# Two-layer decoder step on one core: the head gates at the end of the recurrence load into the places of finished chunks, and the prompt's last state leaves on SyncE's queue right behind its last sum

## The chip, the cores and the metric

The kernel runs on one NeuronCore of a Trainium2 chip. The metric is device time in microseconds of one execution. The kernel before took 2952.51 us, the median of three runs (2949.12, 2952.51 and 2954.06 us). Each engine works through its own list of instructions in order: TensorE (PE, with its weight loads shown apart as PEld), VectorE (DVE), ScalarE (ACT) and GpSimd (POOL). DMAs are issued by SyncE (SP), ACT and POOL, and in the trace an engine's issuing side is written SPq or ACTq.

## What is computed

One inference step of a two-layer decoder for a prompt of 1024 tokens (with 16 meta tokens ahead of it) and for 8 samples of 8 tokens, with the same weights. Layer one is an mLSTM, a recurrence over chunks of tokens whose state is a matrix `C` and a vector `n` per head; layer two is attention with forget gates; each is followed by a SwiGLU network. The change lies where layer one's recurrence ends and its output projection begins:

```python
def mlstm_chunk(state, inp):
    C, n, m = state
    ...
    h = num / jnp.maximum(jnp.abs(den), jnp.exp(-m_t))[..., None]
    ...
    C_new = w_c[..., None, None] * C + jnp.einsum('bhs,bhsk,bhsv->bhkv', w_g, k, v)
    n_new = w_c[..., None] * n + jnp.einsum('bhs,bhsk->bhk', w_g, k)
    return (C_new, n_new, m_new), h

def mlstm_mixer(xn, C0, n0, m0, lead, w_in, b_ig, b_fg, mh_g, w_out):
    ...
    h, state = mlstm_sequence(q, k, v, li, lf, state0, lead)
    h = rmsnorm(h.transpose(0, 2, 1, 3), mh_g)
    out = (h.reshape(B, T, HV).astype(xn.dtype) * jax.nn.sigmoid(og)) @ w_out
    return out, state
```

The gate `sigmoid(og)` has 8 heads of 128 columns. The last `C` and `n` of the prompt are outputs of their own, `p_C` and `p_n`.

## The kernel before, in words

**Tiling.** The 1104 tokens are nine tiles: tile 0 holds the 64 sample tokens and the 16 meta tokens, tiles 1 to 8 hold 128 prompt tokens each. Three tiles make a group t (0, 1, 2; 336, 384 and 384 tokens), and the name `vA` stands for the three big tiles, one for each group. A float32 product is made of three matmuls, since every operand is split into a high and a low part: ACT casts the high part (L243), DVE subtracts for the low part (L244), PE runs L170, L171 and L172.

**The recurrence** (`recurrence`, L829) goes through chunks i = 0 to 8, one a tile. For each chunk PE makes scores (`sps`, L998), transposes the keys (`kps`, L1004), makes the state's sum (`cp`, L1037, added to `C` by DVE, L1041) and the outputs (`nps`, L1099 and L1103, copied out by DVE's `den`, L1061, and by ACT into `vA`, L1069). Between these steps `f(n)` runs pieces of other work, above all the projection of the gates (`gates_out`): its results go through ACT's sigmoid into tiles `stg` (three buffers) and out to DRAM as `ogD`. At i = 6 that work is used up (`f(1000)`), and from then on the filler `g` is one head of the gating: a call of `gate` (L666) takes one pair (t, h), group 0 first, and runs `gate_head`: three PE transposes of the normed output into PSUM (`ghps`, L1198, two buffers), a multiplication with the gate by DVE (L1199), ACT's cast and DVE's subtraction into the operands `x0h`/`x0l` (group 0) or `x1h`/`x1l` (group 1). DVE works in order, so a head's multiplication holds up all DVE work behind it.

Chunks 7 and 8 have five such calls each: heads (0,0) to (0,4) and then (0,5) to (0,7), (1,0), (1,1). The gate of a head is loaded from `ogD` by POOL (L663) into a tile `ogc`, which is one of the three `stg` buffers, and is kept up to three heads ahead. Since the loads run ahead, the recurrence also loads heads (1,2) and (1,3), which it doesn't gate.

**Its end.** After chunk 8's outputs `last_state` (L904) issues four DMAs on ACT's queue: `p_C` and `p_n`, for each half a of the partitions. `p_n` writes single float32 elements: its source is one column of `C` (64 partitions by 4 elements). Then ACT and DVE norm group 2 (`norm_heads`, L1171 to L1182).

**The output projection** (`mlp`, L377) comes next. Unit (t, m) is 24 matmuls (`pops`) that make 128 output columns m for group t, and DVE adds it into the residual stream (L433), which POOL loads from DRAM into `vA` as soon as that group's heads are transposed (L398, `vA<-hD`). Units (0,0), (0,1) and (0,2) come first, each with two heads of group 1 behind it: (1,2) and (1,3) after the first, (1,4) and (1,5) after the second, and so on. Their gates are loaded again by a second set made by `heads`, into the `ny` buffers of a pool of `mlp` (three buffers, name `ogc` too). That pool takes over memory that the recurrence held, `C` among it. The weights are loaded by SP: columns 0 to 2 ready split (`wo`, L411), column 3 raw (`woraw`, L418) and columns 4 to 7 raw into two `slot` tiles (L418); ACT and DVE split the raw ones.

**What sets the order.** PE's order is fixed by hand throughout. In the recurrence DVE, ACT and POOL are in the order of the code too. SP, and the others in `mlp`'s first part, are ordered by the scheduler. A DMA may also wait for the semaphore of an earlier DMA that it shares a counter with; such a wait stands in the trace like any other.

Of the kernel before, what the change touches and what calls it, by code (L numbers as in the profile page):

```python
# [7 lines left out]
F32 = mybir.dt.float32  # L8
# [8 lines left out]
P = 128  # L17
# [10 lines left out]
NT = len(TT)  # L28
GRP = [(0, 1, 2), (3, 4, 5), (6, 7, 8)]
TS = [(TT[g[0]][0], TT[g[-1]][1]) for g in GRP]  # L30
SL = max(b - a for a, b in TS)
HA, DK, DV = 8, 64, 128
# [477 lines left out]
def _add(cls):  # L510
    def deco(f):
        setattr(cls, f.__name__, f)
        return f

    return deco
# [44 lines left out]
@_add(Net)  # L560
def phase_a(self, vt):
    nc, I, O = self.nc, self.I, self.O
    w_in = I["w_in_a"][0]
    qkD = self.dram.tile([8, P, T], F32, name="qkD")
    ogD = self.dram.tile([8, P, T], F32, name="ogD")
    v = lambda i: vt[i // 3][:, i % 3 * HA * (DV + 1) : (i % 3 + 1) * HA * (DV + 1)].rearrange(
        "p (h d) -> p h d", h=HA)
    with ExitStack() as c3:
        kp = c3.enter_context(self.pool("kA"))
        gates = kp.tile([P, NT, 16], F32, name="gates")  # L570
        tm = kp.tile([P, NT, 104], F32, name="tmA")
        den = kp.tile([P, NT, HA], F32, name="den")
        ssq = kp.tile([P, NT, HA], F32, name="ssqA")
        self.fin = (tm, den, ssq)
        for i in range(NT):
            nc.gpsimd.memset(v(i)[:, :, DV : DV + 1], 1.0)
        nc.gpsimd.memset(gates, 0.0)
        nc.gpsimd.memset(tm[:, 0, :], 0.0)
        nc.gpsimd.memset(den, 1.0)
        nc.gpsimd.memset(ssq, 1.0)  # L580
        st = c3.enter_context(self.pool("stA", bufs=3))
        with ExitStack() as cw, self.pool("ppA0", bufs=4, space=PSUM) as pp:
            self.wpools(cw, 3, 4)
            self.load_x()
            for c in (3, 0, 1, 2):
                c0 = 2 * HA * DK + 256 * c

                def evac(i, m, ps):
                    nc.scalar.copy(v(i)[:m, 2 * c : 2 * c + 2, :DV], ps[:m, :256].rearrange("p (h d) -> p h d", h=2))
                    if c == 3:  # L590
                        nc.scalar.copy(gates[:m, i, :], ps[:m, 256:272])

                self.tm_proj([w_in[:, c0 : c0 + 256]] + ([w_in[:, 3072:3088]] if c == 3 else []), None, pp, "mm0", 4,
                             evac)

        pp = c3.enter_context(self.pool("ppA", bufs=2, space=PSUM))

        self.wpools(c3, 2, 3, side="left")
        self.cache_prep()


        self.woD = []
        for m in range(3):
            d = self.dram.tile([P, 2, KT, P], F32, name=f"woD{m}")
            for z, y in enumerate(self.load_w([I["w_out_a"][0][:, m * P : (m + 1) * P]])):
                nc.gpsimd.dma_start(d[:, z], y.bitcast(F32))
            self.woD.append(d)

        def qk_out():

            for m in range(8):
                wh, wl = self.load_w([w_in[:, m * P : (m + 1) * P]])
                for t, (t0, t1) in enumerate(TS):
                    n = t1 - t0
                    ps = pp.tile([P, 512], F32, name=self.uid("mmA"), tag="mmA")
                    self.fm_cols(ps[:, :n], wh, wl, t)
                    s = st.tile([P, SL], F32, name=self.uid("stg"), tag="stg")
                    nc.scalar.activation(s[:, :n], ps[:, :n], AF.Copy, scale=DK ** -0.5 if m < 4 else 1.0)
                    nc.gpsimd.dma_start(qkD[m, :, t0:t1], s[:, :n])
                    yield  # L620

        with self.pool("rowsA") as rp, self.pool("rowsAp", bufs=2, space=PSUM) as rpp, \
                self.tc.manual_schedule(engines={mybir.EngineType.PE}):
            prep = self.rec_prep(kp, gates, rp, rpp)
            next(prep)
            for x, _ in enumerate(qk_out()):
                if x in (1, 3, 8):
                    next(prep, None)

        def gates_out():  # L630

            get = lambda m, later=None: self.load_w([w_in[:, (16 + m) * P : (17 + m) * P]], later=later)
            ws = [get(0)]
            later = []
            for m in range(8):
                wh, wl = ws[m]
                for t, (t0, t1) in enumerate(TS):
                    n = t1 - t0
                    ps = pp.tile([P, 512], F32, name=self.uid("mmA"), tag="mmA")
                    xh, xl = self.X[t]  # L640
                    if t == 1 and m < 7:
                        ws.append(get(m + 1, later if m else None))
                    for k in range(KT):
                        if k == 6 and later:
                            later.pop()()
                        self.mm3(ps[:, :n], wh[:, k, :], wl[:, k, :], xh[:, k, :], xl[:, k, :], k == 0, k == KT - 1)
                        if k == KT - 1:
                            s = st.tile([P, SL], F32, name=self.uid("stg"), tag="stg")
                            nc.scalar.activation(s[:, :n], ps[:, :n], AF.Sigmoid)
                            nc.gpsimd.dma_start(ogD[m, :, t0:t1], s[:, :n])  # L650
                        yield

        left = {t: list(range(HA)) for t in range(3)}

        def heads(pp, tag, op):
            ready = []
            todo = [(t, h) for t in (0, 1, 2) for h in left[t]]

            def ahead():
                if todo:  # L660
                    t, h = todo.pop(0)
                    og = op(self.uid("ogc"))
                    nc.gpsimd.dma_start(og[:, : TS[t][1] - TS[t][0]], ogD[h, :, TS[t][0] : TS[t][1]])  # L663
                    ready.append(og)

            def gate(t):  # L666
                if not left[t]:
                    return False
                while todo and len(ready) < 3:
                    ahead()  # L670
                self.gate_head(t, left[t].pop(0), v, ready.pop(0), pp, tag)
                return True
            return gate

        self.recurrence(kp, self.rec, v, qkD, gates_out(),
                        lambda: heads(pp, "mmA", lambda n: st.tile([P, SL], F32, name=n, tag="stg")))
    return heads


# [149 lines left out]
def recurrence(self, kp, rec, v, qkD, fill, gate):  # L829


    nc, I, O = self.nc, self.I, self.O
# [7 lines left out]
    C = [kp.tile([P, 4, DV + 1], F32, name=f"C{a}") for a in range(3)]  # L840
    E = mybir.EngineType
    with ExitStack() as cr, self.pool("recAp", bufs=2, space=PSUM) as pp:
# [5 lines left out]
        sets = {1: r0}  # L848
# [19 lines left out]
        with self.pool("rec2") as sets[2], self.pool("rec1", bufs=2) as rp, self.pool("rec3") as sets[0]:  # L868
            R, N = N, load(2)
            f(10)  # L870
            self.chunk_scores(1, R, rp, *args, f)
            self.chunk_decay(2, N, tm, cap)
            N["exp"]()
            g, norm = f, iter(())
            gate = gate()
            for i in range(1, NT):
                N2 = load(i + 2) if i + 2 < NT else None
                if i + 1 < NT:
                    f(12 if i == 1 else 3)
                    self.chunk_scores(i + 1, N, rp, *args, f)  # L880
                next(norm, None)
                g(2)
                self.chunk_state(i, R, *args, wcP, g)
                if N2:
                    self.chunk_decay(i + 2, N2, tm, cap)
                next(norm, None)
                self.chunk_out(i, R, rp, *args, den, ssq, g, exp=N2 and N2["exp"])
                if i == NT - 1:
                    self.last_state(C[i % 2])
                for _ in norm:  # L890
                    pass
                norm = self.norm_heads(i // 3, v, rp) if i % 3 == 2 else iter(())
                if i == 6:

                    f(1000)
                    g = lambda n: gate(0) or gate(1)
                R, N = N, N2
            order.close()
            for _ in norm:
                pass  # L900


@_add(Net)
def last_state(self, C):  # L904

    nc, O = self.nc, self.O
    for a in range(2):
        cs = C[a * 64 : a * 64 + 64]
        nc.scalar.dma_start(O["p_C"][0, 0, a::2].rearrange("j k v -> k j v"), cs[:, :, :DV])
        nc.scalar.dma_start(O["p_n"][0, 0, a::2].rearrange("j k -> k j").unsqueeze(2), cs[:, :, DV:])  # L910


@_add(Net)
# [1622 lines left out]
```

## Time and profile before

| | |
|---|---|
| median of three runs | 2952.51 us |
| profiled execution, its own time | 2952.6 us |
| span of its trace | 2950.9 us |
| mean granted TensorE clock | 0.985 |
| PE busy | 2830.5 us (96%) |
| DVE, ACT, POOL busy | 57%, 39%, 28% |
| DMA | 464.83 MB, mean 158 GB/s |

Times in rows of the trace count from the start of the span. In a timeline row stand start, duration, engine, line, operation, what it writes and reads, and in brackets how long the engine was idle just before and what ended that. A row of waits has the total in us, how often, and the longest one. A row of windows has for a stretch the busy time of PE, PEld, DVE, ACT and POOL with the number of instructions, then the granted clock, the busy share of the DMA engines and GB/s. The stretch that matters here lies between 422 us, where the gates' projection ends, and 480 us, where the output projection runs without stops.

### The profile page before, as it was taken

The numbers are of one execution on the slowest core, as the hardware profiler recorded it, in microseconds if no ns is written. First come the engines' busy times: TensorE is split into PE (matmuls) and PEld (weight loads), VectorE is DVE, ScalarE is ACT, GpSimd is POOL, SyncE is SP. The second block draws the span as 40 slices with busy tenths as digits, with TensorE's granted clock in tenths as the row PEclk, the third lists the DMA queues.
The fourth block names the chain that finished last, engine by engine and source line by source line (L and its number), as shares of the span: only waits on it lengthen the run. The fifth ranks groups of instructions, "written<-read, shape, count | busy, mean of one in ns | idle before, by whom it ended". The sixth has DMA issues, their size and how long they took to land.

```text
span 2950.9 us, 53409 instructions
## 1 busy us (share of the span) xinstructions
PE 2830.5 (96%) x20709; PEld 2707.7 (92%) x20709; DVE 1686.3 (57%) x3292; ACT 1151.0 (39%) x2103; POOL 825.6 (28%) x1230
## 2 busy tenths in 40 slices
PE   8999987999999999999999999999999999999998
PEld 7999876999999999989999888777899999999998
DVE  5032554776766655754355442677467676665565
ACT  5222453332222234443344443777433222224343
POOL 2011232322322311114353200455232322331122
PEclk9999998999999999999999999999999999999999
DMA  8153545334444375655344575534324454436574
GB/s 260 36 138 89 142 134 147 110 121 149 153 152 148 122 241 187 199 181 173 119 161 141 199 279 201 185 128 150 120 77 132 144 165 142 143 123 221 190 249 149
DMA packets 382760, 464.83 MB, mean 158 GB/s; under 512 B 38626, under 2 KB 303802, under 8 KB 381482
## 3 DMA queue, kind: packets, MB, share of 16 engines
q1 hardware_dynamic: 339970, 323.41, 34.5%
q0 software_dynamic: 37776, 135.42, 14.1%
q8 instruction: 163, 2.67, 0.4%
q10 hardware_dynamic: 4760, 2.57, 0.4%
q14 instruction: 91, 0.75, 0.1%
HBM read 325.02 MB, written 136.29 MB: 156 GB/s over the span
## 4 chain that ended last, share of the span: by engine, by line
PE 76%; DVE 6%; ACT 3%; issue 3%; DMA 2%; POOL 1%; SPq 0%; ACTq 0%; DVEq 0%; POOLq 0%
PE m L1256 22%; PE dps L1571 15%; PE fps L172 4%; PE fps L171 4%; PE fps L170 4%; PE tmps L170 3%; PE tmps L171 3%; PE tmps L172 3%; PE pops L172 2%; PE pops L170 2%; PE pops L171 2%; PE sp L2323 1%; DVE s L2327 1%; PE op L2410 1%; PE bps L170 1%
## 5 line engine op out<-in xcount | busy, mean ns | idle before, releaser
L244 DVE TENSOR_TENSOR slot<-slot,slot 128x1024 fp32r<-128x1024 f32 (+1 forms) x152 | 191.9, 1264 | 123.7 <-ACT slot L243 123.6
L243 ACT CAST slot<-slot 128x1024 fp32r<-128x1024 f32 (+1 forms) x152 | 152.8, 1007 | 188.5 <-PE dps L1571 84.4
L172 PE MATMUL fps<-x0h,slot 128*128 128x336 f32 x688 | 218.2, 317 | 1.6 <-DVE slot L244 1.6
L170 PE MATMUL fps<-x0h,slot 128*128 128x336 f32 x688 | 218.4, 317 | 0.0
L171 PE MATMUL fps<-x0l,slot 128*128 128x336 f32 x688 | 217.4, 316 | 0.0
L1256 PE MATMUL m<-x2h,slot 128*128 128x384 f32 x704 | 193.7, 336 | 0.0
L1256 PE MATMUL m<-x1h,slot 128*128 128x384 f32 x672 | 184.7, 336 | 0.0
L172 PEld LDWEIGHTS fps<-x0h,slot 128*128 128x128 f32 x688 | 129.1, 188 | 2.1 <-DVE slot L244 2.1
L170 PEld LDWEIGHTS fps<-x0h,slot 128*128 128x128 f32 x688 | 129.3, 188 | 0.6 <-ACT slot L243 0.3
L171 PEld LDWEIGHTS fps<-x0l,slot 128*128 128x128 f32 x688 | 129.5, 188 | 0.3
L1256 PEld LDWEIGHTS m<-x2h,slot 128*128 128x128 f32 x704 | 128.5, 188 | 0.0
L1256 PEld LDWEIGHTS m<-x1h,slot 128*128 128x128 f32 x672 | 122.5, 188 | 0.0
L1571 PE MATMUL dps<-T_1h,slot 128*128 128x384 f32 x448 | 119.3, 340 | 2.4 <-ACT T_1h L243 2.4
L1571 PE MATMUL dps<-T_2h,slot 128*128 128x384 f32 x448 | 119.0, 341 | 0.7 <-ACT T_2h L243 0.7
L1256 PE MATMUL m<-x2l,slot 128*128 128x384 f32 x352 | 118.5, 337 | 0.0
L244 DVE TENSOR_TENSOR slot<-vA,slot 128x1024 fp32r<-128x1024 f32 x59 | 83.6, 1417 | 54.8 <-ACT slot L243 54.8
L244 DVE TENSOR_TENSOR slot<-Ht,slot 128x1024 fp32r<-128x1024 f32 x59 | 83.6, 1418 | 54.5 <-ACT slot L243 54.5
L1256 PE MATMUL m<-x1l,slot 128*128 128x384 f32 x336 | 112.8, 336 | 0.0
L316 POOL TENSOR_TENSOR ns<-ns,nq 128x384 f32<-128x384 f32 (+1 forms) x68 | 75.0, 1104 | 133.0 <-ACT nq L314 130.7
L1256 PE MATMUL m<-T_2h,slot 128*128 128x384 f32 x352 | 97.8, 338 | 1.9 <-DVE slot L244 1.9
L2350 ACT ACTIVATE s<-s,nb 128x272 f32<-128x272 f32 (+7 forms) x126 | 98.9, 786 | 0.0
L1256 PE MATMUL m<-T_4h,slot 128*128 128x384 f32 x352 | 97.8, 338 | 0.0
(767 smaller groups left out, 9173.1 us busy)
## 6 DMA issues: line engine op xcount, KB each, us to landing
slot<-in_w_down SPq DMA_DIRECT2D x48, 512.0 KB, 4.6
slot<-in_w_gate_up SPq DMA_DIRECT2D x36, 512.0 KB, 4.3
ws<-in_w_down SPq DMA_DIRECT2D x88, 192.0 KB, 2.9
sD<-ws SPq DMA_DIRECT2D x88, 192.0 KB, 2.2
kp<-in_cache_k SPq DMA_DIRECT2D x32, 512.0 KB, 5.8
vp<-in_cache_v SPq DMA_DIRECT2D x32, 512.0 KB, 5.1
hr<-hB_T POOLq DMA_DIRECT2D x40, 384.0 KB, 5.0
vA<-in_w_gate_up SPq DMA_DIRECT2D x26, 512.0 KB, 3.9
```

Of the source, the lines that this page charges most:

```text
L170: mm(ps, sh, mh, start=first, stop=False)
L171: mm(ps, sh, ml, start=False, stop=False)
L172: mm(ps, sl, mh, start=False, stop=last)
L243: self.nc.scalar.copy(hi, src)
L244: self.nc.vector.tensor_tensor(out=lo, in0=src, in1=hi.bitcast(F32), op=ALU.subtract)
L316: (nc.vector if x >= late else nc.gpsimd).tensor_tensor(out=s, in0=s, in1=sq, op=ALU.add)
L1256: nc.tensor.matmul(u.ps[b], w[p][:, k], x[q][:, k], start=first and k == i == 0, stop=k == 3 and i == 2, skip_group_check=True)
L1571: nc.tensor.matmul(o, p[:, k, ms], q[:, k], start=fresh and k == x == 0, stop=last and k == nk - 1 and x == 2, skip_group_check=True)
L2323: nc.tensor.matmul(ps[z][:, :n], a[r, qs], b[r, at : at + n], start=(y == 0), stop=(y == 2))
L2327: nc.vector.tensor_tensor_reduce(out=ss[z, u][:, at + o : at + e], in0=ps[z][:, o:e], in1=diag[x][:, z] if y else ncb[:, z, at + o : at + ...
L2350: nc.scalar.activation(ss[z, u], ss[z, u], AF.Exp, bias=nb[:, z : z + 1], accum_out=sm[:, u, z : z + 1])
L2410: mm(po[ds[z], :256], vr[:, j0 + x, ds[z]], th[:, x, z], start=(j0 + x == 0), stop=False)
```

## The change

Lines in the changed kernel are 2 lower down in `heads` and up to 18 lower down from `recurrence` on (L663 is L665, L909 and L910 are L927 and L928, L1041 is L1059, L1199 is L1217).

- At i = 6 and i = 7, behind the chunk's outputs, the places of the chunk's `qk` and `eb` tiles are taken over: a new tile of the same tag, halved, gives two places for gates, so four places an iteration, named `ogqk` and `ogeb`. `gate(-1)` loads into all free places and gates nothing.
- In the recurrence `heads` is given this list of places in the place of the `stg` buffers. It loads whenever a place is free, a used place comes free one head later, and exactly ten heads are loaded (`some`).
- `last_state` runs behind chunk 8's `chunk_state`, and its four DMAs are issued by SP.

```diff
-        def heads(pp, tag, op):
-            ready = []
-            todo = [(t, h) for t in (0, 1, 2) for h in left[t]]
+        left[-1] = [None]
+
+        def heads(pp, tag, op=None, some=None):
+
+            ready, used = [], []
+            todo = [(t, h) for t in (0, 1, 2) for h in left[t]][:some]
 
             def ahead():
                 if todo:
                     t, h = todo.pop(0)
-                    og = op(self.uid("ogc"))
+                    og = op(self.uid("ogc")) if callable(op) else op.pop(0)
                     nc.gpsimd.dma_start(og[:, : TS[t][1] - TS[t][0]], ogD[h, :, TS[t][0] : TS[t][1]])
                     ready.append(og)
 
             def gate(t):
                 if not left[t]:
                     return False
-                while todo and len(ready) < 3:
+                while todo and (len(ready) < 3 if callable(op) else op):
                     ahead()
-                self.gate_head(t, left[t].pop(0), v, ready.pop(0), pp, tag)
+                if t < 0:
+                    return False
+                og = ready.pop(0)
+                self.gate_head(t, left[t].pop(0), v, og, pp, tag)
+                if not callable(op):
+
+                    used.append(og)
+                    if len(used) > 1:
+                        op.append(used.pop(0))
                 return True
             return gate
 
         self.recurrence(kp, self.rec, v, qkD, gates_out(),
-                        lambda: heads(pp, "mmA", lambda n: st.tile([P, SL], F32, name=n, tag="stg")))
+                        lambda places: heads(pp, "mmA", places, 10))
...
-            gate = gate()
+            places = []
+            gate = gate(places)
...
                 self.chunk_state(i, R, *args, wcP, g)
+                if i == NT - 1:
+                    self.last_state(C[i % 2])
...
                 self.chunk_out(i, R, rp, *args, den, ssq, g, exp=N2 and N2["exp"])
-                if i == NT - 1:
-                    self.last_state(C[i % 2])
...
                 norm = self.norm_heads(i // 3, v, rp) if i % 3 == 2 else iter(())
+                if i in (6, 7):
+
+                    for x in ("qk", "eb"):
+                        y = sets[i % 3].tile([P, 1024], F32, name=f"og{x}{i}", tag=x,
+                                             bufs=2 if x == "eb" and i == 7 else None)
+                        places += [y[:, z : z + SL] for z in (0, 512)]
+                    gate(-1)
...
-        nc.scalar.dma_start(O["p_C"][0, 0, a::2].rearrange("j k v -> k j v"), cs[:, :, :DV])
-        nc.scalar.dma_start(O["p_n"][0, 0, a::2].rearrange("j k -> k j").unsqueeze(2), cs[:, :, DV:])
+        nc.sync.dma_start(O["p_C"][0, 0, a::2].rearrange("j k v -> k j v"), cs[:, :, :DV])
+        nc.sync.dma_start(O["p_n"][0, 0, a::2].rearrange("j k -> k j").unsqueeze(2), cs[:, :, DV:])
```

PE runs the same instructions in the same order. Three queues change. The first is POOL's, from the last outgoing gate tiles (`ogD<-stg`) to the loads of `mlp`. Before:

```order
L650 DMA ogD<-stg_4437 128x384
L650 DMA ogD<-stg_4465 128x384
L663 DMA ogc_4487<-ogD 128x336
L663 DMA ogc_4489<-ogD 128x336
L663 DMA ogc_4491<-ogD 128x336
L1044 TENSOR_TENSOR C_2807<-C_2806,wcP 128x516
```

The same place of the changed kernel, on to the first load of `mlp` (`ogc_4800`, head (1,2)):

```order
L665 DMA ogqk_4431<-ogD 128x336 x2
L665 DMA ogeb_4432<-ogD 128x336 x2
L650 DMA ogD<-stg_4443 128x384
L650 DMA ogD<-stg_4471 128x384
L1062 TENSOR_TENSOR C_2807<-C_2806,wcP 128x516
L665 DMA ogqk_4431<-ogD 128x336 x2
L665 DMA ogeb_4432<-ogD 128x336 x2
L665 DMA ogqk_4590<-ogD 128x384 x2
L398 DMA vA_98<-hD 128x8x336
L665 DMA ogc_4800<-ogD 128x384
```

Heads (0,0) to (0,3) are now issued ahead of the last two outgoing tiles; (0,4) to (0,7) follow into the same places, and (1,0) and (1,1), which stood behind the load of the residual (`vA_98<-hD`), stand ahead of it.

The second is SP's queue between the ready weights (`wo`) and the first raw slot. Before, `p_C` and `p_n` stood on ACT's queue, between the last square of chunk 8 and the square root of the norm:

```order
L411 DMA wo_321_4755<-woD_1836 128x1024 x2
L411 DMA wo_322_4756<-woD_1845 128x1024 x2
L418 DMA woraw_4753<-in_w_out_a 128x8x128
L418 DMA slot_4734<-in_w_out_a 128x8x128
L418 DMA slot_4735<-in_w_out_a 128x8x128
```

The changed kernel:

```order
L411 DMA wo_310_4746<-woD_1845 128x1024 x2
L418 DMA woraw_4743<-in_w_out_a 128x8x128
L927 DMA out_p_C<-C_2805 64x4x128
L928 DMA out_p_n<-C_2805 64x4x1
L927 DMA out_p_C<-C_2805 64x4x128
L928 DMA out_p_n<-C_2805 64x4x1
L418 DMA slot_4724<-in_w_out_a 128x8x128
L418 DMA slot_4725<-in_w_out_a 128x8x128
```

The four stand behind `woraw` and ahead of the slots.

The third is DVE's, from head (0,7) on (ACT's casts move in the same way). In the changed kernel the split of `woraw` (`wo_306`) stands inside head (0,7), and the first addition to the residual (L433, unit (0,0)) stands ahead of group 2's norm (L1196 to L1200):

```order
L1217 SCALAR_TENSOR_TENSOR ogeb_4432<-ghps_4639,gain,ogeb_4432 128x336
L244 TENSOR_TENSOR wo_306_4742<-woraw_4743,wo_306_4742 128x1024
L244 TENSOR_TENSOR x0l_4494<-ogeb_4432,x0h_4493 128x336
L1217 SCALAR_TENSOR_TENSOR ogqk_4590<-ghps_4648,gain,ogqk_4590 128x384
...
L1193 TENSOR_TENSOR fA_4694<-fA_4694,rd_4693 128x24
L433 TENSOR_TENSOR vA_98<-vA_98,pops_4772 128x336
L1196 RECIPROCAL fA_4694<-fA_4694 128x24
L1197 TENSOR_TENSOR fA_4694<-fA_4694,rd_4693 128x24
L1200 TENSOR_TENSOR vA_100<-vA_100,fA_4694 128x8x128 x3
L1217 SCALAR_TENSOR_TENSOR ogc_4800<-ghps_4806,gain,ogc_4800 128x384
```

Before, that split stood behind heads (1,2) and (1,3) in `mlp`, and the addition stood behind the norm.

## The prediction

> **What bounds the kernel now.** I read the page first, then the windows around the change, then who waits for whom there, and last the rows in order of time. By the page PE is the bound over the whole span. By the windows it isn't where the change lies: two neighbouring stretches of 28.8 and 27.7 us hold 18.46 and 9.44 us of PE work, at a granted clock of about three quarters, and from 500 us on PE is full.
>
> ```profile
> PE 2830.5 (96%) x20709; PEld 2707.7 (92%) x20709; DVE 1686.3 (57%) x3292; ACT 1151.0 (39%) x2103; POOL 825.6 (28%) x1230
> 422.60:451.40 28.80, 18.46 (x148) 14.53 (x148) 12.64 (x30) 9.82 (x33) 8.92 (x15) 0.76 0.60 197
> 451.40:479.10 27.70, 9.44 (x60) 8.50 (x58) 8.94 (x20) 6.57 (x25) 2.14 (x4) 0.75 0.74 140
> 500.00:530.00 30.00, 30.00 (x191) 29.89 (x190) 13.00 (x20) 6.76 (x14) 10.10 (x12) 1.00 0.26 82
> ```
>
> So about 28 us (10.3 and 18.3) are idle PE time, and what removes it should come off the end one for one, since PE is full behind it. The waits of 420 to 535 us name the cause: PE waits for DVE's gate multiplication, DVE for the gate's load, POOL for `p_n`, and SP's weight load for `p_C`.
>
> ```profile
> PE ghps L1198 <- DVE ogc L1199: 25.4, 6, 8.5
> DVE ogc L1199 <- DMA ogc<-ogD: 25.7, 9, 8.6
> POOL ogc L663 <- DMA out_p_n<-C: 11.6, 1, 11.6
> SPq L418 <- DMA out_p_C<-C: 36.1, 2, 34.2
> ```
>
> The timeline gives the places; each row's bracket is the idle time before it. On DVE, the first gate (0,0) waits 6.63 us, (1,0) 4.38 and (1,3), the last row, 8.59:
>
> ```profile
> 433.48 0.57 DVE L1199 SCALAR_TENSOR_TENSOR ogc<-ghps,gain,ogc 128x336 f32<-128x336 f32 x1 [6.63 <-DMA ogc<-ogD]
> 446.56 0.75 DVE L1041 TENSOR_TENSOR C<-C,cp 128x258 f32<-128x258 f32 x2
> 454.87 0.62 DVE L1199 SCALAR_TENSOR_TENSOR ogc<-ghps,gain,ogc 128x384 f32<-128x384 f32 x1 [4.38 <-DMA ogc<-ogD]
> 460.44 0.18 DVE L1175 TENSOR_TENSOR fA<-fA,rd 128x24 f32<-128x24 f32 x1
> 464.61 3.50 DVE L1182 TENSOR_TENSOR vA<-vA,fA 128x1024 f32<-128x1024 f32 x3
> 469.24 0.62 DVE L1199 SCALAR_TENSOR_TENSOR ogc<-ghps,gain,ogc 128x384 f32<-128x384 f32 x1 [0.72 <-DMA ogc<-ogD]
> 478.44 0.62 DVE L1199 SCALAR_TENSOR_TENSOR ogc<-ghps,gain,ogc 128x384 f32<-128x384 f32 x1 [8.59 <-DMA ogc<-ogD]
> ```
>
> PE takes up its work for good at 479.11, right behind the last of these:
>
> ```profile
> 479.11 0.90 PE L1198 MATMUL ghps<-ident,vA 128*128 128x128 f32 x3 [8.30 <-DVE ogc L1199]
> ```
>
> The time that counts is therefore the start of gate (1,3), now 478.44, and the sum below follows DVE to it.
>
> **The change, step by step.**
>
> *Gates (0,0) to (0,3), loaded early.* POOL issues the first gate load behind both outgoing `stg` tiles:
>
> ```profile
> 417.38 0.60 POOL L650 DMA_DIRECT2D ogD<-stg  x1 [6.23 <-ACT stg L649]
> 424.60 1.07 POOL L650 DMA_DIRECT2D ogD<-stg  x2 [6.61 <-ACT stg L649]
> 425.66 0.54 POOL L663 DMA_DIRECT2D ogc<-ogD  x1
> ```
>
> ```profile
> 418.00:422.00 4.00, 4.00 (x24) 4.00 (x24) 1.43 (x2) 3.99 (x15) 0.00 (x0) 1.00 0.11 43
> 426.00:430.00 4.00, 2.83 (x35) 2.34 (x31) 0.85 (x2) 0.00 (x0) 0.20 (x1) 1.00 1.00 332
> 425.66 7.70 DMA ogc<-ogD
> ```
>
> Now four loads go out right behind the row at 417.38, in 2.2 us of POOL's 6.61 idle ones (four by 0.54). Their places are free: chunk 6's `eb` was last read before 417 by its output matmuls. The DMA engines are a tenth busy in 418 to 422 us (first row; the last one is of the chain and used below), so they land before 426. The first gate starts when DVE is free, 6.63 us before 433.48: 426.85. **Term 1: 6.6 us.** Issuing them delays the two outgoing tiles by nothing, because ACT's `stg` ends that wait.
>
> *Gates (0,4) to (0,7), (1,0), (1,1).* Each waits for a place, then for its load beside SP's weight loads. (0,4) can be issued when POOL's `C` is done: DVE's sum of chunk 7 comes 1.5 us behind the first gate, and POOL takes 1.05, so about 430.2. Under the same weight loads the second gate's load took 4.3 us to the start of its multiplication at 436.13:
>
> ```profile
> 431.80 0.54 POOL L663 DMA_DIRECT2D ogc<-ogD  x1 [5.60 <-DMA ogD<-stg]
> 436.13 0.57 DVE L1199 SCALAR_TENSOR_TENSOR ogc<-ghps,gain,ogc 128x336 f32<-128x336 f32 x1 [0.37 <-DMA ogc<-ogD]
> ```
>
> That lands (0,4) at 434.5, where DVE, following the old spacing, wants it at about 434.2. I take no further wait; at worst, at the 7.70 us that the first load took, it costs 3.5. From the first gate to chunk 8's sum DVE took 13.08 us (433.48 to 446.56); 0.56 of it were load waits and a few tenths PE at half clock. I take 12.2. Chunk 8's sum starts at 439.0, ends at 439.8. **Term 2: 0.9 us**, from -3.5 to +1.5.
>
> *Head (1,0).* Its load no longer stands behind the 1344 KB residual, so the 4.38 us go. The split of `woraw` moves in here:
>
> ```profile
> 479.51 1.04 ACT L243 CAST wo<-woraw 128x1024 fp32r<-128x1024 f32 x1
> 480.58 1.23 DVE L244 TENSOR_TENSOR wo<-woraw,wo 128x1024 fp32r<-128x1024 f32 x1
> ```
>
> ```profile
> 463.09 0.38 SPq L418 DMA_DIRECT2D woraw<-in_w_out_a  x1
> ```
>
> ```profile
> 447.32 0.90 POOL L398 DMA_DIRECT2D vA<-hD  x1 [2.55 <-PE ghps L1198]
> ```
>
> It costs DVE 1.2 us in a chain without slack; its load, issued behind `wo` near 426 instead of 463.09, has 14 us for seven loads of 512 KB at the 332 GB/s of 426 to 430 us (11 us). **Term 3: 4.4 less 1.2, 3.2 us.** Behind it `fA` (460.44, end 460.62) ends at 449.9, 10.7 us earlier in all, and POOL issues (1,2), which waited for `fA`:
>
> ```profile
> 460.70 0.54 POOL L663 DMA_DIRECT2D ogc<-ogD  x1 [3.89 <-DVE fA L1175]
> 472.83 1.06 POOL L663 DMA_DIRECT2D ogc<-ogD  x2 [11.59 <-DMA out_p_n<-C]
> ```
>
> *The four output DMAs leave ACT.* They delayed the square root's table load by 2.23 us:
>
> ```profile
> 459.64 0.74 ACTq L909 DMA_DIRECT2D out_p_C<-C  x1
> 461.75 0.64 ACTq L910 DMA_DIRECT2D out_p_n<-C  x1
> 462.42 1.28 ACT L1176 ACT_TABLE_LOAD   x1 [2.23 <-issue]
> 461.75 10.18 DMA out_p_n<-C
> ```
>
> The norm ended 7.5 us behind `fA` (468.11); now 5.3, so 455.2. Ahead of it DVE now adds to the residual (0.5 us) and waits for `vA<-hD`, issued about 7.5 us sooner than 447.32. The DMA view gives for 446 to 460 us what it took alone, in its last column, for 459 to 463 us the gate load beside `p_n`, and then all gate loads together:
>
> ```profile
> vA<-hD POOLq DMA_DIRECT2D x1, 1344.0 KB, 6.9
> ...
> ogc<-ogD POOLq DMA_DIRECT2D x1, 192.0 KB, 8.4
> ...
> DMA to landing us min/median/max: 2.4/3.7/8.4
> ```
>
> The residual would be there at 446.7; beside `p_n` I allow up to 453. Gate (1,2) follows at 456 to 459, by its own load, issued near 450 and 8.4 us under way as now. So (1,2) gains about 12.
>
> *`p_n` goes out sooner.* This sets (1,3). From the first `p_C` issue to the last `p_n` landing (the chain's row: 461.75 and 10.18, so 471.93) are 12.3 us. SP is idle when chunk 8's sum ends, since `woraw` ahead of it is long issued: the 34.2 us that it now waits are for `p_C` itself. So 439.8 and 12.3 give 452.1; POOL's restart takes 0.9 (471.93 to 472.83), the load until (1,3) starts 5.6 (to 478.44): 458.6. The old place had no 1344 KB transfer beside it, the new one has: between nothing and its own 6.9 us more. I take 0.9, near the lower end, as it starts first and half of it should be through. **Gate (1,3) starts at 459.5, 18.9 us sooner.** It is the later of the two chains, by one to three us.
>
> *What goes besides.* Two wasted loads, (1,2) and (1,3) in the recurrence (2 by 0.54 us on POOL), hidden: POOL is idle there. With the split of `woraw` gone, the restart saves 1.2 us on DVE, of which PE's one stall there, 0.82 us, could return; the slots' loads fall due sooner and could cost as much. Zero. Against 2952.6 for the profiled execution, a tenth above the median, 18.9 gives 2933.7; I say **2934**.
>
> The trace already holds a rule that speaks against one half of the change: `p_n`'s two DMAs move 2 KB in all and stay in flight for about ten us, while the DMA engines are 97% busy at 61 GB/s.
>
> ```profile
> 462.00:472.00 10.00, 0.90 (x3) 0.50 (x3) 5.01 (x7) 2.59 (x4) 0.00 (x0) 0.65 0.97 61
> ```
>
> The Trainium skill, "DMA: Bandwidth & Descriptors", section "Issuing engines are not separate DMA queues", says that DMAs from SP, ACT and POOL run on the same 16 engines and interleave, so that another issuing queue saves only issue time. By that rule the move from ACT to SP alone would be worth the 2.23 us above, and the rest of this step comes from the earlier place. Its "Specifications" put transfers under 512 B among those that are read, modified and written; the row agrees that they are slow, and no row shows that mechanism.
>
> **Rivals.** *A: `p_n`'s slow stretch spreads.* It now meets the residual load and gate (1,2). For it: the 8.4 us of a gate load beside it, against a median of 3.7 for all of them. Against it: `woraw`, which lay beside it before, is out of the way. If the pair lands 6 to 12 us later, the end is 2940 to 2946.
>
> *B: no spreading, no wait for the second gates.* With (1,3) bound by the norm, at 456.5, and PE's 0.82 us returned, 23 us go: 2930.
>
> *C: the output isn't earlier.* If `woraw` on SP waited for something late, `p_C` behind it would go out near 463 again, and (1,3) with it: 2952 to 2956, no change. Against it: SP shows no other wait than `p_C` before 463.
>
> *D: slower.* The mechanism is the residual load on DVE's path. L433 now stands ahead of the norm and of every later gate, and if the 1344 KB crawl at the 61 GB/s of the row above for all their length, they take 22 us: 462 for L433 and 467 for (1,2), still a gain. Slower needs (1,3) behind 478.4, so a load or `p_n` that lands after 472, 32 us after issue, against 12.3 seen. At 45 us, say, it is 2966.
>
> **How the numbers follow.** The forecast (2930.5 to 2938) 58%, A 20%, B 12%, C 5%, D 5%, of which 4 are slower. The range leaves out the far half of A, the end of B and all of C and D: 2929 to 2943. A measurement tells changes of over 0.2% (5.9 us) from none, so faster is the first three, 0.90; within 0.2% is C and the rest of D, 0.06; slower is 0.04.
>
> **What would show it.** Right: `ogqk` loads start near 418 and the first L1199 before 428 without a DMA wait; `C` of chunk 8 near 440; the first `p_C` issue on SPq right behind it; POOL's second gate load of `mlp` released by `p_n` near 453; PE's long rows of waits for L1199 down from 25.4 to under 10 us; full PE from about 460. Wrong: an SP wait ahead of `p_C`, a DVE wait at L433 of over 5 us, or a DMA share near one for over 15 us behind 440. If the gain at 480 us is not there at the end, a later stage gave it back, which the full PE rows speak against.

## The result, and the profile after

| | before | changed |
|---|---|---|
| median | 2953.28 us (4 runs, 2949.12 to 2954.89) | 2933.51 us (4 runs, 2933.16 to 2936.93) |
| ratio, 95% interval | 1 | 0.9938, 0.9924 to 0.9952 |
| span of the profiled execution | 2950.9 us | 2931.7 us |
| mean granted clock | 0.985 | 0.988 |

The change makes the kernel faster by 0.6%, 19.8 us by the medians. Nearly all of it comes from one stretch. Its length is read from two rows of the groups by tile (minimum, median and longest in ns, then the first and the last start): from the last start of the first row to the first start of the second. Before:

```profile
L172 PE MATMUL mmA<-x2h,wlo x128: 332/336/522, 148.9 to 422.6; 128*128 128x384 f32 x128
L170 PE MATMUL pops<-x0h,slot x64: 312/316/482, 499.2 to 2112.4; 128*128 128x336 f32 x64
```

After:

```profile
L172 PE MATMUL mmA<-x2h,wlo x128: 332/336/522, 151.0 to 424.6; 128*128 128x384 f32 x128
L170 PE MATMUL pops<-x0h,slot x64: 311/316/482, 482.3 to 2093.5; 128*128 128x336 f32 x64
```

**The stretch** went from 76.6 us (499.2 less 422.6) to 57.7 us: 18.9 us less, of 19.2 in the span. All rows of this execution stand 2.0 us later than before's up to its start (424.6 against 422.6), through something that lies ahead of the change (151.0 against 148.9 in the first row already); a time in square brackets below has these 2.0 us taken off, so that it compares with before and with the prediction.

The two windows of before, and the one behind them that was full before:

```profile
422.60:451.40 28.80, 22.62 (x171) 18.91 (x170) 16.42 (x40) 14.93 (x56) 6.23 (x10) 0.82 0.77 249
451.40:479.10 27.70, 24.31 (x143) 23.55 (x143) 18.54 (x28) 12.34 (x30) 9.47 (x13) 0.88 0.65 194
500.00:530.00 30.00, 28.70 (x171) 28.17 (x169) 18.95 (x26) 7.96 (x14) 11.98 (x11) 1.00 0.29 100
```

PE now works 46.9 of these 56.5 us, where it worked 27.9. The 1.3 us that it is idle from 500 to 530 us are not new: before has them 16.9 us later (28.72 us busy from 516.9 to 546.9). The waits of 420 to 535 us:

```profile
PE ghps L1216 <- DVE ogc L1217: 3.4, 2, 2.7
PE ghps L1216 <- DVE ogeb L1217: 2.4, 1, 2.4
DVE ogc L1217 <- DMA ogc<-ogD: 5.7, 4, 2.7
DVE ogqk L1217 <- DMA ogqk<-ogD: 1.7, 1, 1.7
POOL ogc L665 <- DMA out_p_n<-C: 1.8, 1, 1.8
```

PE's 25.4 us behind the gate's multiplication have shrunk to 3.4 and 2.4 (and 1.1 in two short waits for `ogqk`), DVE's 25.7 behind the gates' loads to 5.7 and 1.7, POOL's 11.6 behind `p_n` to 1.8, and SP's 36.1 behind `p_C` are gone. In order of time, DVE:

```profile
428.80 0.56 DVE L1217 SCALAR_TENSOR_TENSOR ogqk<-ghps,gain,ogqk 128x336 f32<-128x336 f32 x1
438.40 0.57 DVE L1217 SCALAR_TENSOR_TENSOR ogqk<-ghps,gain,ogqk 128x336 f32<-128x336 f32 x1 [1.74 <-DMA ogqk<-ogD]
442.64 0.75 DVE L1059 TENSOR_TENSOR C<-C,cp 128x258 f32<-128x258 f32 x2
446.99 0.61 DVE L1217 SCALAR_TENSOR_TENSOR ogqk<-ghps,gain,ogqk 128x384 f32<-128x384 f32 x1
460.13 0.62 DVE L1217 SCALAR_TENSOR_TENSOR ogc<-ghps,gain,ogc 128x384 f32<-128x384 f32 x1 [1.14 <-DMA ogc<-ogD]
461.68 0.62 DVE L1217 SCALAR_TENSOR_TENSOR ogc<-ghps,gain,ogc 128x384 f32<-128x384 f32 x1 [0.93 <-DMA ogc<-ogD]
```

These are gate (0,0), gate (0,4), chunk 8's sum, (1,0), (1,2) and (1,3). POOL and SP, the chain's DMAs (issue and time in flight), and PE's restart:

```profile
420.11 1.08 POOL L665 DMA_DIRECT2D ogqk<-ogD  x2
443.42 0.61 SPq L927 DMA_DIRECT2D out_p_C<-C  x1
432.21 6.09 DMA ogqk<-ogD
445.44 10.16 DMA out_p_n<-C
456.16 5.44 DMA ogc<-ogD
462.36 0.90 PE L1216 MATMUL ghps<-ident,vA 128*128 128x128 f32 x3 [0.65 <-DVE ogc L1217]
```

The gates' loads go out at 420, `p_C` right behind chunk 8's sum (443.39), `p_n` lands at 455.60, and 0.56 us later POOL issues the load on which (1,3) waits. PE restarts at 462.36 [460.4] instead of 479.11.

### The profile page after: what moved, and what is told of

Its sections match the earlier page's. It is cut to its first block, busy times and chain, and to the rows that moved or that the text cites. A ratio compares the mean times of both kernels' runs of the same rounds, so it can differ in the third digit from the quotient of the medians.

```text
span 2931.7 us, 53400 instructions
## 1 busy us (share of the span) xinstructions
PE 2831.8 (97%) x20709; PEld 2708.8 (92%) x20709; DVE 1686.1 (58%) x3292; ACT 1150.9 (39%) x2103; POOL 826.8 (28%) x1228
## 4 chain that ended last, share of the span: by engine, by line
PE 77%; DVE 6%; ACT 3%; issue 2%; DMA 2%; POOL 1%; DVEq 0%; SPq 0%; POOLq 0%; ACTq 0%
PE m L1274 22%; PE dps L1589 15%; PE fps L172 4%; PE fps L171 4%; PE fps L170 4%; PE tmps L171 3%; PE tmps L170 3%; PE tmps L172 3%; PE pops L172 2%; PE pops L171 2%; PE pops L170 2%; PE sp L2341 1%; PE op L2428 1%; DVE s L2345 1%; PE bps L170 1%
## 5 line engine op out<-in xcount | busy, mean ns | idle before, releaser
L316 POOL TENSOR_TENSOR ns<-ns,nq 128x384 f32<-128x384 f32 (+1 forms) x68 | 76.6, 1126 | 126.3 <-ACT nq L314 124.0
```

Of the source, the lines that this page charges most:

```text
L316: (nc.vector if x >= late else nc.gpsimd).tensor_tensor(out=s, in0=s, in1=sq, op=ALU.add)
```

## The experiments

All are compared by the stretch, since what lies ahead of it and behind it moves by a few us from one execution to the next (its start lies between 421.5 and 427.2 us in the profiles here). Two executions of one kernel differ in the stretch itself too: 57.7 and 59.6 us for the changed kernel, 55.4 and 54.3 for that with six places. So a difference of under 2 us between single executions shows nothing by itself; the text then goes by the rows.

| kernel | median us (runs) | ratio to before, 95% | stretch us |
|---|---|---|---|
| before | | | 76.6 |
| changed | 2933.51 (4) | 0.9924 to 0.9952 | 57.7 |
| e1 gates alone | 2938.02 (4) | 0.9934 to 0.9970 | 64.3 |
| e2 state alone, ACT | 2947.52 (10) | 0.9973 to 0.9992 | 69.4 |
| e2 state alone, SP | 2944.35 (8) | 0.9957 to 0.9982 | 68.1 |
| e3 changed, on ACT | 2937.81 (4) | 0.9920 to 0.9964 | 60.4 |
| e4 without `p_n` | 2935.53 (1) | | 56.5 |
| e5 `p_n` from its own tile | 2938.39 (1) | | 60.5 |
| e6 `p_n` as rows | 2941.53 (4) | 0.9938 to 0.9972 | 59.3 |
| e7 six places | 2933.53 (1) | | 55.4 |
| r1 changed again | 2935.72 (6) | 0.9917 to 0.9945 | 59.6 |
| r2 six places | 2929.52 (6) | 0.9899 to 0.9925 | 54.3 |
| r3 six places, rows | 2934.04 (6) | 0.9922 to 0.9948 | 53.0 |
| r4 r3, residual on SP | 2935.56 (6) | 0.9924 to 0.9951 | 52.9 |

### The two halves of the change

**e1, the gates alone.** `last_state` stands behind `chunk_out` and on ACT again:

```diff
-                if i == NT - 1:
-                    self.last_state(C[i % 2])
...
                 self.chunk_out(i, R, rp, *args, den, ssq, g, exp=N2 and N2["exp"])
+                if i == NT - 1:
+                    self.last_state(C[i % 2])
```

> The gates' loads in the places of done chunks, with the prompt's last state on ACT's queue behind chunk_out as before. The measure is the stretch from the start of the last mmA matmul to the first pops matmul on a slot: 76.6 us before, 57.7 after. Theory (the start of (1,3) follows the landing of p_n, and the gates bring p_n sooner only as far as fA ends sooner): fA ended 8.9 us sooner after the change, so p_C goes out near 450.6 instead of 459.6, and the stretch is 67.6 us (66 to 69.5), the profiled span some 9 us under before's. Rival 1 (the gates' waits were the whole of it, p_n is hidden anyway): 58 to 60 us. Rival 2 (p_n's place fixes the restart whatever the gates do): 75 to 77 us.

64.3 us, a gain of 12.3, over the 7 to 10.6 that were expected, but far from both rivals. `p_C` went out at 452.04, 1.6 us of which are a later start (424.2): at 450.4, as forecast. The difference is in the last load. Its chain:

```profile
454.15 10.06 DMA out_p_n<-C
464.76 2.62 DMA ogc<-ogD
```

Here SP had issued two slot loads at 450.97, ahead of `p_n`, and they had moved by 460; so the load of (1,3) was alone and took 2.62 us, where it took 5.53 before and 5.44 in the changed kernel, with slot loads beside it.

**e2, the state alone, on ACT.** Before, with `last_state` called behind `chunk_state`:

```diff
                 self.chunk_state(i, R, *args, wcP, g)
+                if i == NT - 1:
+                    self.last_state(C[i % 2])
```

> The prompt's last state alone at the new place (behind its last sum), on ACT's queue, gates loaded as before. Theory: chunk 8's sum ends at 447.3 as before, the last p_n lands 12.3 us behind the first p_C issue, near 460.5, and POOL's load and (1,3) could follow at 467; but the norm, 2.2 us sooner without the issues ahead of the table load, ends at 465.9, and (1,2) and (1,3) stand behind it, so (1,3) at 467 to 469: the stretch is 66 us (65 to 68). Rival 1 (p_n is hidden anyway; only the gates' loads count): 74 to 77 us. Rival 2 (the two parts don't overlap at all, so that this one gives the whole 18.9 less the gates' 9): 66.7 us, told apart from the theory only by which row ends last: by the theory (1,3) waits for the norm and not for its load. If both parts are worth 9 to 11 us each, they add up to 18 to 22 against the 18.9 of both.

69.4 us, a gain of 7.2: 1.4 less than the low end. (1,2) follows the norm, as the theory said, but for 0.4 us for its load. The norm is late: from chunk 8's sum to `fA` are 18.6 us, where before takes 13.9. The rows show two things, the four issues on ACT between two gates' casts, and loads (rows (0,6), (0,7), (1,0), (1,1)):

```profile
450.16 0.56 DVE L1199 SCALAR_TENSOR_TENSOR ogc<-ghps,gain,ogc 128x336 f32<-128x336 f32 x1
454.14 0.56 DVE L1199 SCALAR_TENSOR_TENSOR ogc<-ghps,gain,ogc 128x336 f32<-128x336 f32 x1
460.47 0.62 DVE L1199 SCALAR_TENSOR_TENSOR ogc<-ghps,gain,ogc 128x384 f32<-128x384 f32 x1 [4.72 <-DMA ogc<-ogD]
464.37 0.62 DVE L1199 SCALAR_TENSOR_TENSOR ogc<-ghps,gain,ogc 128x384 f32<-128x384 f32 x1 [2.00 <-DMA ogc<-ogD]
```

From (0,6) to (0,7) are 3.98 us, where the changed kernel takes 1.65. But the loads of (1,0) and (1,1) are now in flight beside `p_n`, for 10.07 and 9.90 us, and DVE waits 4.72 and 2.00 us for them; before, (1,0) waited 4.38 and (1,1) not at all. (1,0)'s load was issued right behind the sum, so its wait would have covered the issues on ACT; they delayed the issue of (1,1)'s load. How much of the late norm is each one's, this run doesn't tell. And SP was held up although the outputs were not on its queue, by a `wo` load that waits for an output's landing:

```profile
SPq L411 <- DMA out_p_C<-C: 33.3, 1, 33.3
```

No data ties the two: they share a counter. In the trace both DMAs report on one semaphore (103), and the `wo` load waits on it first, as `woraw` and `p_C` did before the change (105; 34.2 us). The two halves, 12.3 and 7.2, add up to 19.5, against 18.9 together.

**e2, the state alone, on SP.** The same edit, and `nc.sync` for `nc.scalar`.

> The last state alone at the new place on SP's queue, gates loaded as before. Here the schedule puts the four output DMAs ahead of the six wo loads and woraw on SP. Theory (a queue is served in order): wo's 3 MB go out only behind chunk 8's sum, some 20 us later than before, and land beside p_n and the residual, near 455 to 465; the first wo matmuls and with them the residual additions and the norm wait for them, and the stretch is 68 to 80 us: most or all of the state part's 10 us is given back. The gates' loads have the DMA engines to themselves until then, so the first one takes 2 to 4 us instead of 7.7. Rival (a waiting DMA doesn't hold up those behind it on SP): as with ACT's queue, 65 to 68 us.

68.1 us, at the expected range's edge. SP's queue holds the weights up as expected (its first row is SP's, the second of the waits):

```profile
446.19 12.08 SPq L411 DMA_DIRECT2D wo<-woD  x6
PE pops L170 <- DMA wo<-woD: 10.6, 1, 10.6
```

PE waited 10.6 us for `wo`. That this is no slower than on ACT's queue (1.3 us in the stretch is within what executions differ by) goes with the gates: with no weights beside it the first gate's load took 2.85 us in place of 7.70, and chunk 8's sum came 18.8 us behind the start of the stretch, in place of 24.0 (446.56 less 422.6). Here too (1,0) and (1,1) then wait for their loads, 3.67 and 4.78 us, the second one 11.6 us in flight beside `p_n`. So the same line of code, without the early gates, is put at another place by the scheduler and becomes another experiment.

**e3, the changed kernel with the outputs on ACT.** `nc.scalar` for `nc.sync` in `last_state`.

> The changed kernel with the four output DMAs issued by ACT at the new place instead of by SP. Theory (the place counts, the queue only for issue time): four issues of about 0.65 us stand in ACT's chain of the last gates' splits, so fA and what is behind it come 0 to 2.6 us later, p_n lands at most 2 us later: the stretch is 58 to 60.3 us, the span 0 to 2.6 us above the changed kernel's. Rival (the queue counts: on ACT's queue p_n waits for other work as it did before): the stretch is over 64 us.

60.4 us, 2.7 more than the changed kernel (0.8 more than its second execution), hardly over the range, and the rival at 64 is out. But not all of it is issue time. The issues bring `fA` 2.3 us later (31.2 us behind the stretch's start, against 28.9), of which the wait for `p_n` had covered most: gates (1,2) and (1,3) follow the norm, and 0.7 us for their loads, at 37.4 us behind the stretch's start (461.65 less 424.3), against 35.5 and 37.1 in the changed kernel, so the restart is later by less than 1 us. The rest is lost behind it. POOL issues the second residual load 0.4 us ahead of SP's fourth slot load (the second row is of the chain):

```profile
469.24 0.90 POOL L398 DMA_DIRECT2D vA<-hD  x1 [2.53 <-issue]
469.62 11.87 DMA slot<-in_w_out_a
```

The slot takes 11.87 us, and ACT waits 7.7 us for it. In the changed kernel the slot goes first (469.2 against 470.80), and ACT's longest wait for one is 0.4 us.

### What the wait for `p_n` is worth

**e4, without `p_n`.** The `p_n` line of `last_state` is taken out.

> The changed kernel without the two p_n DMAs (p_n is left out of the output). The measure is the stretch from the start of the last mmA matmul to the first pops matmul on a slot, 57.7 us in the changed kernel. Theory (p_n's landing is what (1,3) waits for, 1 to 3 us behind the norm): POOL issues (1,2) and (1,3) together right behind fA, so both gates stand behind the norm's end (459.0, against 461.68 for (1,3) now): the stretch is 56 us (55.3 to 56.5). Rival 1 (another wait is as late, p_n doesn't count): 57.5 to 58. Rival 2 (p_n's ten us slow every load beside it, residual and slots too): below 55.

56.5 us, the top of the range. The two gates do stand right behind the norm, 34.0 us behind the start (460.87 less 426.9) instead of 35.5 and 37.1, so `p_n` is what the last gate waits for. The restart's full gain is larger, 4.6 us at the first matmul of unit (1,0), and most of it goes at the same slot as in e3: the residual load is issued at 468.56, the slot at 468.94.

```profile
468.94 11.29 DMA slot<-in_w_out_a
ACT slot L243 <- DMA slot<-in_w_out_a: 7.4, 2, 7.0
```

**e5, `p_n` out of a tile of its own.**

```diff
+    nc.gpsimd.tensor_copy(self.pn, C[:, :, DV:])
...
-        nc.sync.dma_start(O["p_n"][0, 0, a::2].rearrange("j k -> k j").unsqueeze(2), cs[:, :, DV:])
+        nc.sync.dma_start(O["p_n"][0, 0, a::2].rearrange("j k -> k j").unsqueeze(2), self.pn[a * 64 : a * 64 + 64])
```

> The changed kernel with p_n's column copied by POOL into a small tile of its own, from which the same two slow DMAs go out: nothing that follows waits for them, but they are in flight beside the loads of (1,2) and (1,3). Theory (the wait for p_n is what costs): as without p_n, 55.5 to 56.5 us. Rival (its slowness costs by the loads beside it): (1,3)'s load crawls until p_n has landed near 456, and the stretch is 57.2 to 58 us.

60.5 us: no better than leaving the wait in (57.7 and 59.6). Nothing waits for `p_n` any more, but what goes out beside it crawls. The second window has the restart's place; the last row is of the chain, the load of (1,2):

```profile
452.00:456.00 4.00, 4.00 (x30) 3.99 (x29) 3.18 (x7) 1.85 (x3) 0.55 (x1) 1.00 0.13 29
456.00:460.00 4.00, 0.61 (x4) 0.33 (x3) 1.57 (x2) 0.00 (x0) 1.07 (x2) 0.88 0.71 181
452.38 11.21 DMA ogc<-ogD
```

With two slot loads, (1,2)'s load and `p_n` out, 29 GB/s were moved in 452 to 456 us, and the DMA engines were 13% busy. (1,2)'s load, 192 KB, took 11.21 us, and the second half of `p_C`, issued at 443.2, landed at 456.0. So taking the wait away doesn't pay while `p_n` itself is out.

**e6, `p_n` as four rows.** `self.pn` is a column of 128 by 4, `pr` 4 by 128:

```diff
+    nc.gpsimd.tensor_copy(self.pn, C[:, :, DV])
+    ps = pp.tile([P, P], F32, name="pnp", tag="cps")
+    nc.tensor.transpose(ps[:4, :], self.pn, self.ident)
+    nc.vector.tensor_copy(pr, ps[:4, :])
+    nc.gpsimd.dma_start(O["p_n"][0, 0].rearrange("(j a) k -> j (a k)", a=2), pr)
```

> The changed kernel with p_n turned by PE into four rows of 128 (POOL copies the column, PE transposes it, DVE copies the rows) and written by one DMA of 4 descriptors of 512 bytes; all of the last state goes out on POOL's queue, behind the gates' loads and ahead of the residual load. Theory (p_n is slow because it moves single elements of 4 bytes): it is in flight for 2 to 3 us instead of ten, lands near 449, and p_C, up to 8.8 us in flight, near 453, so (1,3)'s load goes out behind fA: 55.5 to 56.8 us. Rival 1 (a small write is slow whatever its form): p_n 8 us or more in flight, 57 to 58.5. Rival 2 (POOL, waiting for PE's and DVE's part, holds up the residual load): L433 waits, over 58.5.

The rows are for the theory of the element size (sizes, and last the time in flight):

```profile
out_p_C<-C POOLq DMA_DIRECT2D x2, 128.0 KB, 2.7
out_p_n<-pr POOLq DMA_DIRECT2D x1, 2.0 KB, 1.5
```

The same 2 KB land in 1.5 us instead of 10. The queue changed too, from SP's to POOL's, and single elements were not tried on POOL's; but SP's queue isn't slow as such, since the changed kernel's 16 stores of 256 KB on it (`out_y_prompt<-Ht`) take a median of 2.1 us. `p_C` takes 2.7 us with neither `p_n` nor the residual load beside it, 5.4 in e4 beside the residual alone, and 8.8 in the changed kernel beside both; that `p_n` makes the rest isn't shown, since in r3 below it takes 8.3 us with `p_n` in rows, beside a residual load and slot loads. The stretch, 59.3 us, is no shorter than the changed kernel's 57.7 and 59.6, by none of the rivals: DVE waits in its own chain for the transposition, ahead of gate (0,6).

```profile
446.25 0.28 DVE L933 COPY pr<-pnp 4x128 f32<-4x128 f32 x1 [2.24 <-PE pnp L932]
```

From chunk 8's sum to `fA` are 14.3 us (443.25 to 457.54) instead of 10.9.

### The second gates, and further versions

**e7, six places.** At i = 6 the tiles `wb` and `kw` of that chunk become places too:

```diff
+                    if i == 6:
+                        for x in ("wb", "kw"):
+                            y = sets[i % 3].tile([P, 512], F32, name=f"og{x}{i}", tag=x)
+                            places.append(y[:, :SL])
                     gate(-1)
```

> The changed kernel with six places at chunk 6 instead of four (wb and kw of chunk 6 too), so that the loads of gates (0,4) and (0,5) also go out near 422, ahead of the weight loads. Theory (the 6.09 us that (0,4)'s load took beside the weight loads made DVE wait 1.74 us, and all of it reaches the restart): no wait there, chunk 8's sum and p_n 1.7 us sooner, the stretch 56 us (55.5 to 56.5). Rival (the next load in line, (0,6) or (1,0), waits in its place): 57.2 to 58 us.

55.4 us, as expected. (0,4) no longer waits for its load:

```profile
438.99 0.57 DVE L1221 SCALAR_TENSOR_TENSOR ogwb<-ghps,gain,ogwb 128x336 f32<-128x336 f32 x1 [0.53 <-PE ghps L1220]
```

Chunk 8's sum comes 16.4 us behind the start, in place of 18.0.

The last four ran on one chip.

> The changed kernel once more, beside the next three on the same chip. The stretch from the last mmA matmul to the first slot matmul should be 57.7 us again (57 to 58.5), the fourth slot load issued ahead of the second residual load (vA<-hD, 1536 KB), and the time 0.6% under before (0.5 to 0.8).

> Six places at chunk 6, timed. The stretch was 55.4 us against 57.7 in single executions, so 2.3 us or 0.08% should go: 2931 us where the changed kernel gives 2933.5, a difference that rounds of 5 may not resolve. If instead the 2.3 us are given back behind the stretch, both times are alike within 1 us.

The changed kernel's stretch was 59.6 us this time, over what was expected, because two loads took longer: (0,4)'s 6.97 us, so that DVE waited 3.32 us, and (1,2)'s 9.36 us beside `p_n`, so that (1,2)'s load, not (1,3)'s, ended the wait; (1,3)'s landed 0.3 us later.

```profile
441.81 0.57 DVE L1217 SCALAR_TENSOR_TENSOR ogqk<-ghps,gain,ogqk 128x336 f32<-128x336 f32 x1 [3.32 <-DMA ogqk<-ogD]
457.22 9.36 DMA ogc<-ogD
```

Six places gave 54.3 us and the lowest median, 2929.52 against 2935.72 us. The intervals overlap a little (0.9899 to 0.9925, 0.9917 to 0.9945); the stretches, 54.3 and 55.4 against 57.7 and 59.6, two executions each, don't.

> Six places, and p_n as four rows, transposed by PE behind the last gate (1,1) instead of between gates (0,5) and (0,6), with p_C and p_n on POOL's queue. Theory: p_n is 1 to 3 us in flight and lands before fA, (1,2) and (1,3) follow the norm without a wait, PE restarts 2 to 2.6 us sooner than with six places alone; but then the second residual load (1536 KB, POOL) is issued a few tenths of a us ahead of the fourth slot load, as in the two runs in which ACT waited 7 us for that slot, so 3 to 5 us are given back: the stretch is 55.5 to 57.5 us. Rival (that stall had another cause, such as the late release of the slot, and doesn't come here): 52 to 54 us.

> The kernel of the run before with one more edit: the second residual load goes out on SP's queue, where the schedule puts it behind the fourth slot load. Theory (the order of these two transfers is what stalled ACT): the fourth slot lands in about 5 to 7 us, no wait of 7 us, the stretch is 52 to 54.5 us, the time 2927 to 2931, the fastest here. Rival (another cause): as the run before, 55.5 to 57.5. If the residual is needed before it lands (about 10 us behind its issue near 470), its waiter, the addition to vA, shows it, and the gain is lost again.

In r3 the transposition stands behind gate (1,1) and `p_C` and `p_n` on POOL's queue (the edits of e6 and e7, with the transposition in a function called behind `chunk_out`); r4 adds

```diff
-                    load(nc.gpsimd, 1)
+                    load(nc.sync, 1)
```

Both gates then follow the norm with no wait, and the stretch is 53.0 and 52.9 us, the shortest of all. Not all of that need be `p_n`: without the outputs on its queue SP also issues the first slot load at 431.44 us, against 441.74 in r2, so the slots no longer lie beside these gates' loads. The bet on the slot, though, decides nothing: in r3 the fourth slot load was out by 461.06 us and the residual load came at 462.12, so the bad order never came up. That the order of these two costs ACT 7 us rests on e3 and e4 against the others, not on a run made for it. And the times don't follow: 2934.04 and 2935.56 us are no better than the changed kernel's. In the profiles both lose behind the stretch much of what they had won in it: from the first slot matmul to the end of the span are 2449.4 us in the changed kernel (2931.7 less 482.3), 2451.3 in r2, 2452.9 in r3 and 2456.0 in r4. It may be spread alone: over all the profiles here this part lies between 2446.8 (e1) and 2456.0 us, with 2451.7 before. Why is open. Six places alone has the lowest median here; its interval reaches that of r3 and r4.

## Why the prediction was right, step by step

The forecast was 2934, the median 2933.51; the start of gate (1,3) was forecast at 459.5 and came at 461.68 [459.68]. The mechanism was right, but not every term, and that the sum came out this close is luck.

- **What bounds it**: confirmed. The 18.9 us that left the stretch are the difference of the spans but for 0.3, since 2.0 us lost ahead of it and 2.3 won behind it nearly cancel, which is luck too; PE behind it is as full as before.
- **Term 1**: right, gate (0,0) at [426.8], forecast 426.85, without a wait.
- **Term 2** failed: 0.9 us were forecast, 0.8 were lost (chunk 8's sum ended at [441.4], not at 439.8). The step that failed is "That lands (0,4) at 434.5": the load took 6.09 us beside the weights, not the 4.3 of before's second gate. It cost 1.74 us there, 3.32 in r1, within the bound of 3.5; e7 and r2, which load this gate early, got 2.3 and 5.3 us for it.
- **Term 3** was a little small: from chunk 8's sum to (1,0) are 4.35 us instead of 8.31, 4.0 in place of 3.2. It acts on the norm's chain, which came second, and so not on the sum.
- **`p_n`'s chain** was right: 12.18 us from the first `p_C` issue to the last landing (443.42 to 455.60) for 12.3, the restart 0.56 for 0.9, to (1,3) 5.5 for 5.6. The 0.9 us for the residual beside it were not needed. These small errors, 1.4 us in all, paid for the 1.6 us by which chunk 8's sum was late.
- **"It is the later of the two chains"**: shown by e4, and only just: the norm is next, 1.5 to 3 us ahead. In r1 it was (1,2)'s load, by 0.2 us.
- **Nothing for the slots**: right for the changed kernel, but the cover is thin. In e3 and e4 the fourth slot fell behind the residual, and 4.0 and 3.4 us were lost between unit (1,0) and the first slot matmul, which take 9.0 us in the changed kernel.
- **The rule on queues** (the Trainium skill, "DMA: Bandwidth & Descriptors", "Issuing engines are not separate DMA queues"): e3 agrees as to the place. With the four issues on ACT `fA` was 2.3 us later, the size of the 2.23 us of the prediction, from issue time in ACT's chain; the gates' restart was less than 1 us later.
- **Rival A** described something real. In the profiled execution `p_n` didn't get longer (10.16 us for 10.18), but where the residual load itself took 9.5 to 9.8 us instead of 6.9, it did: 12.4 us in r1, 13.1 in e7, 12.6 in r2. And loads beside it got longer, 9.36 us in r1 and 11.21 in e5.
- **Rivals B, C and D** didn't come: ahead of `p_C` SP waited for DVE's sum alone, and L433 waited for no residual. The two wasted loads were not tried by themselves.

## What to carry to other kernels

Where a stretch is a chain, move the start of the chain and look at once at what comes second: here the wait for `p_n`, the norm and a slot load lay within 4 us of each other, so each further gain was partly given back. An output that is written element by element can be turned into rows before it leaves (1.5 us in flight for 10), but where the turning is put matters as much, and no version with it was faster in time here. And after moving a DMA, read where the scheduler put it: one line moved SP's outputs ahead of 3 MB of weights in one kernel and behind them in another.

## What was not expected of the hardware

- Two DMAs of 1 KB in elements of 4 bytes were 10 to 13 us in flight wherever the views give it, on ACT's queue as on SP's. As 4 rows of 512 bytes the same data took 1.5 us.
- While they were in flight, other DMAs were slow without the DMA engines being busy: 29 GB/s at a share of 0.13 in e5. The prediction had read the 97% of before's window as the mark of this state; it isn't one, as a window of the changed kernel shows, in which `p_C` and `p_n` were out and from 451.65 us a slot load:

```profile
450.00:452.00 2.00, 2.00 (x14) 2.00 (x13) 1.45 (x5) 1.59 (x9) 0.00 (x0) 0.94 0.00 0
```

From 450 to 455.6 us that trace has no packet of under 512 bytes, so the single elements were through 5.6 us before `p_n` landed at 455.60. What it and the loads behind it then waited for, no row here tells.
- A load of 512 KB issued 0.4 us behind one of 1536 KB took 11.3 and 11.9 us and landed last (the large one took 9.6 and 10.1). Issued 0.9 to 2.1 us ahead of it, it cost no wait of over 0.8 us; issued 0.7 us ahead, in r1, it took 7.2 us and ACT waited 2.89 us for it.
